# The products of the recurrence that read q ahead of those that read k, and one empty place in the queue of its steps

## The chip, the core and the metric

One core of a Trainium2 chip runs the whole program. The metric is the device time of one execution in microseconds (us), from the first to the last instruction with the little that stands around them; lower is better. The engines work side by side and wait for each other through semaphores: PE is TensorE (matmuls; PEld are its weight loads), DVE is VectorE, ACT is ScalarE, POOL is GpSimd, and SP issues most of the DMAs.

## The reference: what is computed

One layer of a decoder trunk runs for a prompt (256 rows) and for 8 samples of 8 rows (64 rows); they share all weights. The layer projects the normalized input to q, k, v, gates and a pooling branch, runs gated linear attention with 4 heads, merges both branches, projects back, and ends with a SwiGLU feed-forward part. What the change touches is the gated linear attention:

```
b = jnp.cumsum(loga, axis=3)
b_last = b[:, :, :, -1:, :]
qe = q * jnp.exp(b)
ke = k * jnp.exp(-b)
kd = k * jnp.exp(b_last - b)
decay = jnp.exp(b_last[:, :, :, 0, :])
...
att = jnp.where(mask, jnp.einsum('nbhcd,nbhsd->nbhcs', qe, ke), 0.0)
o_intra = jnp.einsum('nbhcs,nbhse->nbhce', att, v)
...
s = dec_n[..., None] * s + jnp.einsum('bhcd,bhce->bhde', kd_n, v_n)
```

## The kernel before

All 320 rows (256 of the prompt, 64 of the samples) stand in the free dimension. Each weight chunk of 128x512 numbers is loaded by SP (`raw`), split into a high part by ACT (`whi`, L159) and a low part by DVE (`wlo`, L160), and each weight tile then takes three matmuls of 320 columns (`mm3`, L198 to L200). `whi` and `wlo` have five buffers each. A projection (`proj`) covers 256 output columns: 96 such matmuls into one PSUM tile of the pool `pmain`, which has two buffers (`ps`, and `psy` for the pooling branch). A PSUM tile comes free when `evac` has copied it into SBUF or added it to what is there (DVE L383 for group 0's gates `mg`). Four more PSUM tiles (`pmisc`, `pm`) serve everything else.

The four heads are done as groups h = 0 to 3. While the projections of group h+1 run on PE, the recurrence of group h is slipped in between them: its steps are functions in a list, and `pump(10)` calls the next ten of them after each projection unit. For group 0 the list is: the gates (`sig0`), four steps of the pooling branch, the first 12 steps of `gla_steps`, the pooling product `s_y`, and the rest. `PSY` is the number of steps ahead of `s_y`. The order of the calls is not the last word: a scheduler then moves instructions on each engine by its own estimates, except where code pins them.

The steps that matter here: `s_gk` makes the log of the gate (ACT L774 to L782, DVE L780 and L783); `s_exp(d)`, d = 0 and 1 for the two halves of a head, sums it over time with six matmuls (L795 and L796, into `pa` and `pb`) and takes nine exponentials on ACT (L800 to L805); `s_prod` multiplies them with q and k on DVE (L811 to L833) and lets POOL copy part of the k products (L816). `s_vstack` stacks v (ACT L841, DVE L843), `s_nat2`, `s_nat3` and `s_kp` transpose on PE (L132, L136). `s_y` multiplies the pooled rows by their weights into two `psy` tiles, which DVE adds at L1090.

q and k of all groups live in one buffer each. So the copy of the next group's q out of PSUM (`evac`, ACT L385) has to wait until DVE has done the last product that reads the old q, and until it is done its PSUM tile is not free. In between, `ada_step` multiplies modulation weights (`w_ada`) in sets of 32 or 48 small matmuls (L250).

Of the kernel before, what the change touches and what calls it, by code (L numbers as in the profile page):

```python
# [15 lines left out]
ALU = mybir.AluOpType  # L16
# [4 lines left out]
P = 128  # L21
TP, NB, LS = 256, 8, 8
TS = NB * LS
T = TP + TS
# [8 lines left out]
OQ, OK_, OV, OOG, OU, OGA, OGB, OAL = 0, 1024, 2048, 4096, 6144, 7168, 9216, 11264  # L33
UEP = PB + TP
UEW = UEP + NB * (PB + LS)
PSY = 12
WB = 5
AB = 3
SLICES = ((0, 2), (2, 4), (4, 8), (8, 12), (12, 16))
# [42 lines left out]
def body(tc, A):  # L82
# [22 lines left out]
    V, S, G, PE = nc.vector, nc.scalar, nc.gpsimd, nc.tensor  # L105
# [222 lines left out]
    def s3(ap):  # L328
        return ap.rearrange("p (b t) -> p b t", t=LS)
# [414 lines left out]
    def w4(shape, dt=F32):  # L744
        return lp.tile(shape, dt, tag="w4", bufs=4, name=nm("w4"))

    def gla_steps(g):
        h = g.h
        st = []
# [39 lines left out]
        def s_exp(d):  # L789
            def f():  # L790
                pa, pb = misc(), misc()
                ds = slice(d * P, (d + 1) * P)
                for ps, rows, s, rhs, a, b in ((pa, P, 0, M0, 0, NM0), (pa, TS, 2, MS, NM0, NM0 + NMS),
                                               (pb, P, 1, M1, 0, NM1)):
                    PE.matmul(ps[:, a:b], lhsT=E["lgh"][:rows, s, ds], rhs=rhs, start=True, stop=False)  # L795
                    PE.matmul(ps[:, a:b], lhsT=E["lgl"][:rows, s, ds], rhs=rhs, start=False, stop=True)  # L796
                EQ, EK, EX = E["EQ"][:, d], E["EK"][:, d], E["EX"][:, d]
                i16 = 1.0 / 16.0
                for dst, sc in ((EQ, i16), (EK, -i16)):
                    S.activation(dst[:, 0:P], pa[:, 0:P], AF.Exp, scale=sc)  # L800
                    S.activation(dst[:, P:2 * P], pb[:, 0:P], AF.Exp, scale=sc)
                    S.activation(dst[:, TP:T], pa[:, NM0:NM0 + TS], AF.Exp, scale=sc)
                S.activation(EX[:, 0:144], pa[:, P:NM0], AF.Exp, scale=i16)
                S.activation(EX[:, 144:416], pb[:, P:NM1], AF.Exp, scale=i16)
                S.activation(EX[:, 416:480], pa[:, NM0 + TS:NM0 + 2 * TS], AF.Exp, scale=i16)  # L805
            return f

        def s_prod():
            EQ, EK, EX, q, k = E["EQ"], E["EK"], E["EX"], g.q, g.k
            for d in range(2):  # L810
                V.tensor_tensor(qeP[:, d, :, 0:LS], s3(EQ[:, d, TP:T]), s3(q[:, d, TP:T]), op=ALU.mult)  # L811
                kk = s3(k[:, d, TP:T])
                V.tensor_tensor(keP[:, d, :, 0:LS], s3(EK[:, d, TP:T]), kk, op=ALU.mult)
                V.tensor_copy(E["dec"][:, d], s3(EQ[:, d, TP:T])[:, :, LS - 1])
            for d in range(2):
                G.tensor_copy(keP[:, d].rearrange("p b (c t) -> p b c t", t=LS)[:, :, 1:4, :],  # L816
                              keP[:, d, :, 0:LS].unsqueeze(2).broadcast_to([P, NB, 3, LS]))
            V.tensor_tensor(EX[:, :, 416:480], EX[:, :, 416:480], k[:, :, TP:T], op=ALU.mult)
            kdP = E["kdP"] = w4([P, 2, NB, 32], F32R)
            for d in range(2):  # L820
                kd4 = kdP[:, d].rearrange("p b (c t) -> p b c t", t=LS)
                kd = s3(EX[:, d, 416:480]).unsqueeze(2).broadcast_to([P, NB, 2, LS])
                V.tensor_copy(kd4[:, :, 0:2, :], kd)
                V.tensor_tensor(kd4[:, :, 2:4, :], kd, kd4[:, :, 0:2, :].bitcast(F32), op=ALU.subtract)
            V.tensor_tensor(EQ[:, :, 0:TP], EQ[:, :, 0:TP], q[:, :, 0:TP], op=ALU.mult)
            V.tensor_tensor(EK[:, :, 0:TP], EK[:, :, 0:TP], k[:, :, 0:TP], op=ALU.mult)
            kq = w4([P, 2, 2, P])
            E["kdA"], E["q2"] = kq[:, 0], kq[:, 1]
            V.tensor_tensor(EX[:, :, 0:P], EX[:, :, 0:P], k[:, :, 0:P], op=ALU.mult)
            V.tensor_tensor(EX[:, :, 144:272], EX[:, :, 144:272], k[:, :, P:TP], op=ALU.mult)  # L830
            V.tensor_tensor(E["q2"], EX[:, :, 272:400], q[:, :, P:TP], op=ALU.mult)
            for d in range(2):
                V.tensor_scalar(E["kdA"][:, d], EX[:, d, 0:P], EX[:, d, 399:400], None, op0=ALU.mult)  # L833

# [113 lines left out]
        def s_load(gg, d):  # L948
            def f():
                t = lp.tile([P, 4, DV], F32, tag="S0", bufs=2, name=nm("S0"))  # L950
                nc.gpsimd.dma_start(t, A["state_gla"][0, 4 * gg:4 * gg + 4, h, d * P:(d + 1) * P, :]
                                    .rearrange("b p e -> p b e"))
                E["S0", gg, d] = t
            return f
# [36 lines left out]
        def s_norm():  # L991
# [11 lines left out]
            V.reciprocal(rs, rs)  # L1003
            for e in range(4):
                V.scalar_tensor_tensor(o[:, e], o[:, e], GNG[:, e:e + 1], rs, op0=ALU.mult, op1=ALU.mult)
        st += [s_load(0, 0), s_load(0, 1), s_wa2, s_gk, s_exp(0), s_exp(1), s_prod, s_vstack, s_nat2, s_nat3, s_kp(0), s_attP,
               s_inter(0), s_oback(0)]
        for d in range(2):
            st += [s_state(0, d, 0), s_state(0, d, 2), s_load(1, d)]
# [90 lines left out]
        return f  # L1100

    queue = []

    def pump(n):
        for _ in range(min(n, len(queue))):
# [278 lines left out]
```

## Time and profile before

| | |
|---|---|
| median of 3 runs | 1969.22 us (1968.83 to 1969.24) |
| the profiled execution | 1966.94 us, of which the span of instructions is 1965.2 us |
| PE busy | 1938.0 us, 99% of the span |
| DVE, ACT, POOL busy | 1020.0, 826.4, 137.4 us |
| mean granted clock of PE | 0.996 of full speed |

PE is the engine to look at: what the others do matters only where PE stands still for it, or runs at the lower clock. A busy PE is counted by modelled ends of its matmuls, so the spacing of starts says more than a busy share. The profiled execution is 2.3 us shorter than the median of the runs.

### The profile page before, as it was taken

How to read it: one execution, taken by the hardware profiler on the slowest of the kernel's cores; microseconds unless marked ns; L12 is line 12 of the kernel's file. 1: busy time of each engine (PE TensorE's matmuls, PEld its weight loads, DVE VectorE, ACT ScalarE, POOL GpSimd, SP SyncE). 2: the span in 40 equal slices, each digit the busy share in tenths (PEclk: the TensorE clock that was granted, in tenths of full speed). 3: DMA queues.
4: the chain of work that ended last, by engine and by line, in shares of the span. 5: the costliest groups of instructions: out<-in, count | busy, mean ns of one | idle time of the engine just before them, and what ended most of it. 6: DMA issues, size and time to landing. Idle time of an engine off the chain costs nothing.

```text
span 1965.2 us, 37340 instructions
## 1 busy us (share of the span) xinstructions
PE 1938.0 (99%) x15068; PEld 1850.7 (94%) x15068; DVE 1020.0 (52%) x1912; ACT 826.4 (42%) x1493; POOL 137.4 (7%) x257
## 2 busy tenths in 40 slices
PE   9999999999999999999999999999999999999997
PEld 6899998898999999889999999999999999999997
DVE  3666575565556544774574444444444444444554
ACT  4333374463345433643353333333333434344443
POOL 1012220111011101010030000000000000000000
PEclk9999999999999999999999999999999999999998
DMA  9988645765976786679656765444444444444443
GB/s 320 398 274 267 193 143 181 260 229 201 324 240 207 277 267 217 207 253 329 205 186 195 224 195 187 148 152 143 154 151 150 150 150 151 150 150 144 148 140 94
DMA packets 324607, 400.84 MB, mean 204 GB/s; under 512 B 13545, under 2 KB 264681, under 8 KB 324097
## 3 DMA queue, kind: packets, MB, share of 16 engines
q1 hardware_dynamic: 312002, 357.68, 56.4%
q0 software_dynamic: 12432, 40.78, 5.7%
q8 instruction: 118, 1.93, 0.4%
q14 instruction: 55, 0.45, 0.1%
HBM read 373.96 MB, written 24.67 MB: 203 GB/s over the span
## 4 chain that ended last, share of the span: by engine, by line
PE 92%; ACT 1%; DMA 1%; DVE 1%; issue 0%; POOL 0%; POOLq 0%; DVEq 0%; ACTq 0%
PE ps L198 27%; PE ps L199 27%; PE ps L200 27%; PE pm L250 4%; PE pm L132 1%; PE pm L963 1%; PE pm L984 1%; DMA raw<-w_ada 1%; PE pm L928 1%; PE pm L917 0%; PE pm L795 0%; PE pm L136 0%; PE pm L796 0%; PE pm L863 0%; PE psy L198 0%
## 5 line engine op out<-in xcount | busy, mean ns | idle before, releaser
L160 DVE TENSOR_TENSOR wlo<-raw,whi 128x512 fp32r<-128x512 f32 x948 | 653.9, 694 | 770.2 <-ACT whi L159 766.8
L159 ACT CAST whi<-raw 128x512 fp32r<-128x512 f32 x948 | 584.7, 621 | 972.1 <-PE ps L199 869.2
L198 PE MATMUL ps<-hh,whi 128*128 128x320 f32 x1408 | 440.8, 314 | 3.2 <-ACT hh L572 1.0
L200 PE MATMUL ps<-hh,wlo 128*128 128x320 f32 x1408 | 438.5, 312 | 0.1
L199 PE MATMUL ps<-hl,whi 128*128 128x320 f32 x1408 | 437.4, 311 | 0.7 <-DVE hl L588 0.7
L198 PE MATMUL ps<-h2h,whi 128*128 128x320 f32 x1408 | 435.8, 310 | 0.0
L199 PE MATMUL ps<-h2l,whi 128*128 128x320 f32 x1408 | 434.9, 309 | 0.8 <-DVE h2l L1254 0.8
L200 PE MATMUL ps<-h2h,wlo 128*128 128x320 f32 x1408 | 434.8, 309 | 0.0
L198 PEld LDWEIGHTS ps<-hh,whi 128*128 128x128 f32 x1408 | 264.3, 188 | 19.5 <-issue 11.9
L199 PEld LDWEIGHTS ps<-hl,whi 128*128 128x128 f32 x1408 | 264.4, 188 | 7.1 <-issue 4.6
L200 PEld LDWEIGHTS ps<-hh,wlo 128*128 128x128 f32 x1408 | 264.4, 188 | 6.2 <-issue 4.9
L198 PEld LDWEIGHTS ps<-h2h,whi 128*128 128x128 f32 x1408 | 264.1, 188 | 2.4 <-issue 2.2
L199 PEld LDWEIGHTS ps<-h2l,whi 128*128 128x128 f32 x1408 | 264.3, 188 | 1.1 <-DVE h2l L1254 1.1
L200 PEld LDWEIGHTS ps<-h2h,wlo 128*128 128x128 f32 x1408 | 264.3, 188 | 0.0
L198 PE MATMUL ps<-ah,whi 128*128 128x320 f32 x704 | 218.5, 310 | 0.0
L200 PE MATMUL ps<-ah,wlo 128*128 128x320 f32 x704 | 217.7, 309 | 0.0
L199 PE MATMUL ps<-al,whi 128*128 128x320 f32 x704 | 217.6, 309 | 0.0
L199 PEld LDWEIGHTS ps<-al,whi 128*128 128x128 f32 x704 | 132.2, 188 | 0.0
L198 PEld LDWEIGHTS ps<-ah,whi 128*128 128x128 f32 x704 | 132.2, 188 | 0.0
L200 PEld LDWEIGHTS ps<-ah,wlo 128*128 128x128 f32 x704 | 132.2, 188 | 0.0
L250 PE MATMUL pm<-raw,scT 128*32 128x128 f32 (+1 forms) x2688 | 99.5, 290 | 0.3 <-DMA raw<-w_ada 0.3
L250 PEld LDWEIGHTS pm<-raw,scT 128*32 128x32 f32 x2688 | 71.0, 109 | 21.1 <-issue 13.6
(321 smaller groups left out, 1581.4 us busy)
## 6 DMA issues: line engine op xcount, KB each, us to landing
raw<-w_ada SPq DMA_DIRECT2D x192, 512.0 KB, 6.4
raw<-w_gu SPq DMA_DIRECT2D x176, 512.0 KB, 3.5
raw<-w_in SPq DMA_DIRECT2D x173, 512.0 KB, 4.1
raw<-w_down SPq DMA_DIRECT2D x79, 512.0 KB, 3.3
S<-state_gla POOLq DMA_DIRECT2D x16, 1024.0 KB, 8.9
o_gs<-S POOLq DMA_DIRECT2D x16, 1024.0 KB, 5.9
raw<-w_o SPq DMA_DIRECT2D x32, 512.0 KB, 5.3
raw<-w_down SPq DMA_DIRECT2D x15, 256.0 KB, 2.6
```

The source lines that it names most:

```text
L132: PE.transpose(out, in_, ident[:k, :k])
L159: S.copy(hi, raw)
L160: V.tensor_sub(lo, raw, hi.bitcast(F32))
L198: PE.matmul(ps, lhsT=whi, rhs=xhi, start=start, stop=False)
L199: PE.matmul(ps, lhsT=whi, rhs=xlo, start=False, stop=False)
L200: PE.matmul(ps, lhsT=wlo, rhs=xhi, start=False, stop=stop)
L250: ins = PE.matmul(ps[32 * j:32 * j + 32, 0:w], lhsT=scT[:, k, :], rhs=raws[j], start=k == 0 if start is None else start, stop=k == KT - 1 ...
L928: PE.matmul(pt, lhsT=E["kdn"][:, s, d * P:(d + 1) * P], rhs=E["vn"][:, s], start=s == 0, stop=s == 1)
L963: PE.matmul(pt[32 * j:32 * j + 32, :], lhsT=qeP[:, d, 4 * gg + j, :], rhs=E["S0", gg, d][:, j], start=False, stop=d == 1, tile_position=(0 ...
L984: PE.matmul(pt, lhsT=kpz[:, j, d * P:(d + 1) * P], rhs=E["vp"][:, gg], start=True, stop=True)
```

## The change

In `s_prod` the copy of the decays (`dec`) and the four products with q are called first, then those with k. The list of steps of every group gets an empty step (`pause`) behind `s_gk`, and `PSY` goes from 12 to 13, so that `s_y` of group 0 keeps its place among the steps. Since the tenth step of group 0's list was `s_exp(0)`, this step, and one at each later border of ten, is now called one projection later. For the groups 1 to 3 the whole list is called between two projections, so there the empty step moves nothing by itself.

```diff
@@ -33,7 +33,7 @@
 OQ, OK_, OV, OOG, OU, OGA, OGB, OAL = 0, 1024, 2048, 4096, 6144, 7168, 9216, 11264
 UEP = PB + TP
 UEW = UEP + NB * (PB + LS)
-PSY = 12
+PSY = 13
 WB = 5
 AB = 3
 SLICES = ((0, 2), (2, 4), (4, 8), (8, 12), (12, 16))
@@ -807,11 +807,16 @@
 
         def s_prod():
             EQ, EK, EX, q, k = E["EQ"], E["EK"], E["EX"], g.q, g.k
+            kq = w4([P, 2, 2, P])
+            E["kdA"], E["q2"] = kq[:, 0], kq[:, 1]
             for d in range(2):
+                V.tensor_copy(E["dec"][:, d], s3(EQ[:, d, TP:T])[:, :, LS - 1])
                 V.tensor_tensor(qeP[:, d, :, 0:LS], s3(EQ[:, d, TP:T]), s3(q[:, d, TP:T]), op=ALU.mult)
+            V.tensor_tensor(EQ[:, :, 0:TP], EQ[:, :, 0:TP], q[:, :, 0:TP], op=ALU.mult)
+            V.tensor_tensor(E["q2"], EX[:, :, 272:400], q[:, :, P:TP], op=ALU.mult)
+            for d in range(2):
                 kk = s3(k[:, d, TP:T])
                 V.tensor_tensor(keP[:, d, :, 0:LS], s3(EK[:, d, TP:T]), kk, op=ALU.mult)
-                V.tensor_copy(E["dec"][:, d], s3(EQ[:, d, TP:T])[:, :, LS - 1])
             for d in range(2):
                 G.tensor_copy(keP[:, d].rearrange("p b (c t) -> p b c t", t=LS)[:, :, 1:4, :],
                               keP[:, d, :, 0:LS].unsqueeze(2).broadcast_to([P, NB, 3, LS]))
@@ -822,13 +827,9 @@
                 kd = s3(EX[:, d, 416:480]).unsqueeze(2).broadcast_to([P, NB, 2, LS])
                 V.tensor_copy(kd4[:, :, 0:2, :], kd)
                 V.tensor_tensor(kd4[:, :, 2:4, :], kd, kd4[:, :, 0:2, :].bitcast(F32), op=ALU.subtract)
-            V.tensor_tensor(EQ[:, :, 0:TP], EQ[:, :, 0:TP], q[:, :, 0:TP], op=ALU.mult)
             V.tensor_tensor(EK[:, :, 0:TP], EK[:, :, 0:TP], k[:, :, 0:TP], op=ALU.mult)
-            kq = w4([P, 2, 2, P])
-            E["kdA"], E["q2"] = kq[:, 0], kq[:, 1]
             V.tensor_tensor(EX[:, :, 0:P], EX[:, :, 0:P], k[:, :, 0:P], op=ALU.mult)
             V.tensor_tensor(EX[:, :, 144:272], EX[:, :, 144:272], k[:, :, P:TP], op=ALU.mult)
-            V.tensor_tensor(E["q2"], EX[:, :, 272:400], q[:, :, P:TP], op=ALU.mult)
             for d in range(2):
                 V.tensor_scalar(E["kdA"][:, d], EX[:, d, 0:P], EX[:, d, 399:400], None, op0=ALU.mult)
 
@@ -1003,7 +1004,7 @@
             V.reciprocal(rs, rs)
             for e in range(4):
                 V.scalar_tensor_tensor(o[:, e], o[:, e], GNG[:, e:e + 1], rs, op0=ALU.mult, op1=ALU.mult)
-        st += [s_load(0, 0), s_load(0, 1), s_wa2, s_gk, s_exp(0), s_exp(1), s_prod, s_vstack, s_nat2, s_nat3, s_kp(0), s_attP,
+        st += [s_load(0, 0), s_load(0, 1), s_wa2, s_gk, pause, s_exp(0), s_exp(1), s_prod, s_vstack, s_nat2, s_nat3, s_kp(0), s_attP,
                s_inter(0), s_oback(0)]
         for d in range(2):
             st += [s_state(0, d, 0), s_state(0, d, 2), s_load(1, d)]
@@ -1100,6 +1101,9 @@
         return f
 
     queue = []
+
+    def pause():
+        pass
 
     def pump(n):
         for _ in range(min(n, len(queue))):
```

How the scheduler places it is seen at two places of group 0's recurrence. The first is on PE, after the gate projection `ps_3000`: the names are PSUM tiles and what is multiplied into them, `cumr` the matrix of the sums and `w` the log of the gate.

```order
 L199 MATMUL ps_3000<-hl_2626,whi_3019 128x320
 L200 MATMUL ps_3000<-hh_106,wlo_3020 128x320
-L795 MATMUL pm_3326<-cumr,w_490_3309 128x272
-L796 MATMUL pm_3326<-cumr,w_491_3310 128x272
-L795 MATMUL pm_3326<-cumr,w_490_3309 128x128
-L795 MATMUL pm_3327<-cumr,w_490_3309 128x400
-L796 MATMUL pm_3327<-cumr,w_491_3310 128x400
 L198 MATMUL ps_3036<-hh_103,whi_3039 128x320
 L199 MATMUL ps_3036<-hl_2524,whi_3039 128x320
```

The five sums of `s_exp(0)` that stood between the projections `ps_3000` and `ps_3036` are gone; a sixth, 48 matmuls on, is gone too. All twelve sums of both halves now stand at the second place, ahead of and between the pooling products. There PE had, before the change (in brackets the engines whose semaphores a row waits for):

```order
L198 MATMUL psy_3621<-dh_3289,whi_3641 128x320
L199 MATMUL psy_3621<-dl_3290,whi_3641 128x320
L200 MATMUL psy_3621<-dh_3289,wlo_3642 128x320
L198 MATMUL psy_3622<-dh_3289,whi_3625 128x320 [waits PE_49,Activation_49]
L199 MATMUL psy_3622<-dl_3290,whi_3625 128x320
L200 MATMUL psy_3622<-dh_3289,wlo_3626 128x320
```

and has now (`pm_3523` is `pb` of the second half):

```order
L198 MATMUL psy_3621<-dh_3289,whi_3641 128x320
L199 MATMUL psy_3621<-dl_3290,whi_3641 128x320
L200 MATMUL psy_3621<-dh_3289,wlo_3642 128x320
L795 MATMUL pm_3523<-cumr,w_490_3309 128x400 [waits PE_49,Activation_49]
L796 MATMUL pm_3523<-cumr,w_491_3310 128x400
L198 MATMUL psy_3622<-dh_3289,whi_3625 128x320 [waits DVE_49]
L199 MATMUL psy_3622<-dl_3290,whi_3625 128x320
L200 MATMUL psy_3622<-dh_3289,wlo_3626 128x320
```

The last two sums stand between the two pooling tiles, and the second tile `psy_3622` no longer waits for ACT but for DVE, so it takes the buffer that `psy_3621` leaves. DVE had at this place, in the second half of the products:

```order
L811 TENSOR_TENSOR qeP<-EQK_3323,q_248 128x8x8 [waits Activation_49]
L814 COPY dec_3324<-EQK_3323 128x8
L813 TENSOR_TENSOR keP<-EQK_3323,k_249 128x8x8 [waits Activation_49]
L829 TENSOR_TENSOR EX_3325<-EX_3325,k_249 128x2x128 [waits Activation_49]
L818 TENSOR_TENSOR EX_3325<-EX_3325,k_249 128x2x64 [waits Activation_49]
L825 TENSOR_TENSOR EQK_3323<-EQK_3323,q_248 128x2x256 [waits Activation_49]
L826 TENSOR_TENSOR EQK_3323<-EQK_3323,k_249 128x2x256 [waits Activation_49]
L830 TENSOR_TENSOR EX_3325<-EX_3325,k_249 128x2x128 [waits Activation_49]
L823 CAST w_531_3548<-EX_3325 128x8x16 [waits DVE_49]
L823 CAST w_531_3548<-EX_3325 128x8x16
L831 TENSOR_TENSOR w_532_3555<-EX_3325,q_248 128x256
L833 TENSOR_SCALAR w_532_3555<-EX_3325 128x128 x2
```

and has now:

```order
L813 COPY dec_3324<-EQK_3323 128x8 [waits Activation_49]
L814 TENSOR_TENSOR qeP<-EQK_3323,q_248 128x8x8
L819 TENSOR_TENSOR keP<-EQK_3323,k_249 128x8x8 [waits Activation_49]
L831 TENSOR_TENSOR EX_3325<-EX_3325,k_249 128x2x128 [waits Activation_49]
L823 TENSOR_TENSOR EX_3325<-EX_3325,k_249 128x2x64 [waits Activation_49]
L1091 SCALAR_TENSOR_TENSOR mg_111<-psy_3621,vec,mg_111 128x320 [waits PE_49]
L1091 SCALAR_TENSOR_TENSOR mg_111<-psy_3621,vec,mg_111 128x320
L834 TENSOR_SCALAR w_531_3539<-EX_3325 128x128 [waits DVE_49]
L815 TENSOR_TENSOR EQK_3323<-EQK_3323,q_248 128x2x256 [waits Activation_49]
L830 TENSOR_TENSOR EQK_3323<-EQK_3323,k_249 128x2x256 [waits Activation_49]
L816 TENSOR_TENSOR w_531_3539<-EX_3325,q_248 128x256 [waits Activation_49]
L828 CAST w_532_3551<-EX_3325 128x8x16 [waits DVE_49]
```

The two instructions that empty `psy_3621` (L1091, L1090 before) now stand ahead of the large products with q, and the last product that reads q (L816, L831 before) stands ahead of the casts (L828, L823 before) and of one product with k, behind which it stood. ACT had, in the same stretch,

```order
L801 ACTIVATE EQK_3323<-pm_3523 128x128 [waits PE_49]
L801 ACTIVATE EQK_3323<-pm_3523 128x128
L804 ACTIVATE EX_3325<-pm_3523 128x272
L841 CAST w_533_3561<-v_250 128x8x8 x8
L385 ACTIVATE q_3343<-ps_3347 128x640 [waits DVE_49]
L159 CAST whi_3735<-raw_3717 128x512 [waits PE_49,Activation_49]
```

and has now

```order
L801 ACTIVATE EQK_3323<-pm_3523 128x128 [waits PE_49]
L801 ACTIVATE EQK_3323<-pm_3523 128x128
L804 ACTIVATE EX_3325<-pm_3523 128x272
L842 CAST w_533_3561<-v_250 128x8x8 x8
L159 CAST whi_3724<-raw_3706 128x512 [waits DVE_49,PE_49]
L385 ACTIVATE q_3326<-ps_3330 128x640 [waits DVE_49]
```

The copy of q out of PSUM (L385) stands behind one more split of weights (L159), whose buffer is the one that `psy_3622` reads.

## Rows read from the trace of the kernel before

**Rows 1.** The page: engine totals, and two groups by line (busy us, mean ns).

```profile
PE 1938.0 (99%) x15068; PEld 1850.7 (94%) x15068; DVE 1020.0 (52%) x1912; ACT 826.4 (42%) x1493; POOL 137.4 (7%) x257
L160 DVE TENSOR_TENSOR wlo<-raw,whi 128x512 fp32r<-128x512 f32 x948 | 653.9, 694 | 770.2 <-ACT whi L159 766.8
L159 ACT CAST whi<-raw 128x512 fp32r<-128x512 f32 x948 | 584.7, 621 | 972.1 <-PE ps L199 869.2
```

**Rows 2.** PE's waits in the whole span: us in total, times, longest.

```profile
PE psy L198 <- ACT q L385: 2.3, 1, 2.3
PE pm L796 <- DVE w L783: 1.4, 1, 1.4
PE pm L795 <- ACT w L782: 0.8, 1, 0.8
```

**Rows 3.** Timeline of PE, 268 to 280 us (start, us, instruction).

```profile
268.57 0.31 PE L200 MATMUL ps<-hh,wlo 128*128 128x320 f32 x1
271.69 0.31 PE L198 MATMUL ps<-hh,whi 128*128 128x320 f32 x1
278.58 0.31 PE L200 MATMUL ps<-hh,wlo 128*128 128x320 f32 x1
279.07 0.41 PE L198 MATMUL ps<-hh,whi 128*128 128x320 f32 x1
```

**Rows 4.** Timeline of POOL and DVE, 267 to 272 us.

```profile
267.89 1.55 POOL L401 TENSOR_TENSOR og<-og,sg 128x640 f32<-128x640 f32 x1 [4.16 <-ACT sg L397]
268.35 1.64 DVE L160 TENSOR_TENSOR wlo<-raw,whi 128x512 fp32r<-128x512 f32 x1 [1.86 <-ACT whi L159]
270.51 0.81 DVE L383 SCALAR_TENSOR_TENSOR mg<-ps,mg 128x640 f32<-128x640 f32 x1
```

**Rows 5.** Windows (length, busy by engine, PEclk, DMA share, GB/s).

```profile
272.00:276.00 4.00, 4.00 (x29) 4.00 (x29) 2.22 (x5) 3.96 (x8) 0.50 (x1) 1.00 0.72 223
311.00:314.00 3.00, 3.00 (x14) 3.00 (x14) 2.54 (x13) 0.86 (x2) 0.00 (x0) 0.59 0.12 44
314.00:316.00 2.00, 2.00 (x14) 2.00 (x14) 2.00 (x4) 0.39 (x1) 0.00 (x0) 0.76 0.59 158
```

**Rows 6.** Timeline of PE, 305 to 315 us.

```profile
305.36 0.39 PE L795 MATMUL pm<-cumr,w 128*128 128x272 f32 x1
306.64 0.31 PE L198 MATMUL psy<-dh,whi 128*128 128x320 f32 x1
308.26 0.30 PE L200 MATMUL psy<-dh,wlo 128*128 128x320 f32 x1
310.89 0.42 PE L198 MATMUL psy<-dh,whi 128*128 128x320 f32 x1 [2.33 <-ACT q L385]
314.80 0.46 PE L198 MATMUL ps<-hh,whi 128*128 128x320 f32 x1
```

**Rows 7.** Timeline of ACT and DVE, 305 to 315 us.

```profile
306.28 0.28 ACT L800 ACTIVATE EQK<-pm 128x128 f32<-128x128 f32 x1 [0.49 <-PE pm L796]
307.09 0.51 ACT L801 ACTIVATE EQK<-pm 128x128 f32<-128x128 f32 x2
307.68 1.33 ACT L841 CAST w<-v 128x64 fp32r<-128x64 f32 x8
307.88 0.68 DVE L825 TENSOR_TENSOR EQK<-EQK,q 128x512 f32<-128x512 f32 x1
309.69 0.41 DVE L831 TENSOR_TENSOR w<-EX,q 128x256 f32<-128x256 f32 x1
310.13 0.70 ACT L385 ACTIVATE q<-ps 128x640 f32<-128x640 f32 x1 [1.12 <-DVE w L831]
313.99 1.01 DVE L1090 SCALAR_TENSOR_TENSOR mg<-psy,vec,mg 128x320 f32<-128x320 f32 x2 [0.46 <-PE psy L200]
```

**Rows 8.** Waits of the SP queue in the whole span.

```profile
SPq L149 <- PE pm L250: 61.1, 71, 3.2
```

**Rows 9.** DMA issues of the page: count, KB, median us to landing.

```profile
raw<-w_in SPq DMA_DIRECT2D x173, 512.0 KB, 4.1
```

## The prediction

> **What bounds the kernel.** I read the page first: PE is busy for 1938.0 us, 99% of the span, and no other engine for more than 52% [rows 1]. So only two things can move the time: moments in which PE stands still, and moments in which it runs at its lower clock. The list of PE's waits has three entries in the stretch that the change touches: 2.3 us before the second pooling tile, 1.4 us before a sum of the decays, 0.8 us before the same sums of group 1 [rows 2]. Then the timelines around the two places of group 0, and windows over them for the clock.
>
> At the second place the last matmul of the first pooling tile starts at 308.26 and the first of the second at 310.89 [rows 6]. Twelve matmuls from 306.64 to 308.26 are eleven spacings: 0.147 us each at full clock. So 2.63 - 0.15 = 2.48 us are lost. The chain behind it: PE's sums, ACT's exponentials from 306.28, the DVE products until 310.10 (309.69 + 0.41), the copy of q until 310.83, PE at 310.89 [rows 6, 7]. [...] At the first place PE stood for 1.4 us, and the clock in 272 to 276 stayed at 1.00 [rows 2, 5].
>
> **First place: the sums that leave.** Before, the last matmul of one gate projection starts at 268.57 and the next projection at 271.69, with five sums and the wait of 1.4 us in between [rows 2, 3]. After, nothing stands in between; but the next projection needs the PSUM buffer that DVE empties at L383, and that ends at 270.51 + 0.81 = 271.32 [rows 4]. What comes ahead of it on DVE, ACT and POOL is not changed by the edit. So PE starts at about 271.36 and wins 0.33 us, not 1.4: the wait is renamed, and PE now stands from 268.72 to 271.36, 2.64 us, with no sums to fill it. The lone sixth sum goes too: 279.07 - 278.58 = 0.49 us, against a spacing of 0.15, wins 0.34 [rows 3]. Together 0.67. The supply of weight tiles behind it does not get worse: by the order on ACT, two loads of activation tables between the splits are gone.
>
> **Second place: the sums that arrive.** Count from the first of the twelve sums. Six took 306.64 - 305.36 = 1.28 us [rows 6], so twelve and the first pooling tile (12 x 0.147 = 1.76) keep PE until 4.32. The last two sums stand behind the tile, which therefore ends near 4.0 (an estimate: a third of 1.28 earlier, and the drain).
>
> ACT starts 0.92 after the first sum (306.28 - 305.36) and needs 307.68 - 306.28 = 1.40 for nine exponentials; the second half starts at 2.32. DVE's large products began 1.60 after ACT's start (307.88 - 306.28) [rows 7], so here DVE is through its small ones at 3.92. It then empties the first pooling tile, two instructions of 1.01 us together [rows 7], until 5.05, and the second tile starts: PE waits 5.05 - 4.32 = 0.73, and is done at 6.81.
>
> The copy of q comes later. ACT's last three exponentials need the last sums (4.32, with drain 4.5) and take 307.68 - 307.09 = 0.59; the eight casts of v take 1.33, the split of weights that now stands ahead 0.62, the copy itself 0.70 [rows 1, 7]: 4.5 + 0.59 + 1.33 + 0.62 + 0.70 = 7.74. The q products don't decide: from the first large product to the end of the last one with q were 2.22 us (307.88 to 310.10, [rows 7]), less some 0.4 for what now stands behind, so 5.05 + 1.8 = 6.9, ahead of the copy at 7.04. **The order of q and k, which the change is named after, is worth nothing here**, since ACT is later than DVE. The next projection starts at 7.75 and waits 0.94.
>
> In the same count the kernel before took 314.80 - 305.36 = 9.44 us [rows 6], with six of the sums and with six transposes that now come later. Those ran mostly at the lower clock, 1.05 us from the end of the pooling tile; at full clock at least half of that, I take 0.6. So 7.75 + 0.6 = 8.35, and the place wins 1.09, the fall of the clock that goes with the gap included. Bounds of the waits: 0 if DVE and ACT are faster than counted; the old 2.48 if they are as late as before.
>
> **Group 1.** Ahead of its sums stand 39 projection matmuls where 31 stood. Eight times 0.147 is 1.2 us more cover for a wait of 0.8 [rows 2]. ACT has one more sigmoid in front of the gate, hidden in part. Between 0 and 0.8 I take 0.75. The groups 2 and 3 have no PE wait that the new order could take away; there nothing is counted, since the q copy is a whole group away.
>
> **The clock at the first place.** This is the disputed cost: 0 or 1.71. Idle for 2.3 us was followed by a fall, 1.4 us was not [rows 2, 5]. A standstill of 2.64 between starts is nearest to the one of 2.48, so I take the fall: it moves from the second place, where the two waits are short and have work between them, to the first.
>
> [...] The subtraction at 268.35 took 1.64 us, against 694 ns on average, while POOL multiplied from 267.89 for 1.55 us [rows 1, 4]. POOL's two copies of the k products now follow each other closer to the critical chain; I count nothing for it, since the chain of [rows 7] already had one beside it; if a product is stretched as this one was, that is 1.64 - 0.69 = 0.95 us more (a rival below). [...]
>
> **The sum.** 0.67 + 1.09 + 0.75 - 1.71 = 0.8 us faster, against 1966.94 us of the profiled execution: 1966.1. That execution is 2.3 us under the median of the runs, 1969.22, so on the scale of the runs 1968.4. A measurement of this kernel can tell about 0.2%, 3.9 us, from no change; this is inside.
>
> **The rivals.**
> - No fall at either place: gain 2.5, 1966.7 us. For it: 1.4 us did not bring one. Against: the standstill is the longest in the stretch.
> - Falls at both places: 0.9 slower, 1970.1. For it: 0.73 + 0.94 us of waiting lie close together. Against: each alone is shorter than 1.4.
> - Slower by more than can be missed: the sets of modulation matmuls move by up to 36 projection matmuls in group 1 (5.3 us later), and SP, which issues in order, holds the weight loads queued behind theirs. It waited 71 times for such a set, 3.2 us at the longest [rows 8]. A load lands in 4.1 us [rows 9]; 5.3 + 4.1 = 9.4 against a cover of two other buffers, 2 x 24 x 0.147 = 7.1: 2.3 us short for one set. Eight sets move later; two of them decide (4.7 us, 1973.1). Against it: the order of SP's loads moves along with the sets.
> - Faster by more than can be missed: no fall, and ACT and DVE early enough that both waits at the second place are gone: 2.5 + 1.67 = 4.2, 1965.0. Against it: the copy of q stands behind a split that itself waits for the second pooling tile.
> - POOL in the way: one product on the chain is stretched by 0.95 us [rows 1, 4], the time 1969.4. Against it: one such copy ran beside the old chain, and its times are those used here.
> - The change does not do what it says: that is in the sum already; the gain comes from the place in the queue alone.
>
> **Numbers.** My forecast 0.45, no fall 0.23, falls at both 0.13, slow loads 0.08, all waits gone 0.07, POOL in the way 0.04. The first three lie from 1966.7 to 1970.1; with half of either tail and 1 us for how an execution stands to the runs: 1965.4 to 1971.0. Faster by over 0.2%: 0.1 (all waits gone, and a part of no fall); slower by over 0.2%: 0.09; within: 0.81.
>
> **What the profile after would show.** Right: a PE wait for DVE's L383 near 268.7 to 271.4 with the clock low just behind it; waits of under 1 us each before the second pooling tile (for DVE L1091) and before the next projection (for ACT L385), with the clock at 1.00; none before group 1's L795. Wrong: a wait on L385 as long as the old one; a projection that waits for a load; a clock of 1.00 throughout.

## The result, and the profile after

| | before | after |
|---|---|---|
| median of 15 runs | 1968.1 us (1966.47 to 1971.07) | 1972.95 us (1969.83 to 1976.71) |
| ratio, 95% interval | | 1.0023 (1.0016 to 1.003) |
| the profiled execution | 1966.94 us, span 1965.2 | 1973.64 us, span 1971.9 |

The changed kernel is slower by a little more than the 0.2% that a measurement of this kernel can tell, and 1972.95 lies outside the range that was given, 1965.4 to 1971.0. PE is still the whole of it: 1940.3 us busy, where it was 1938.0 [rows 1]. Its waits in the changed kernel (us in total, times, longest), of those that answer to [rows 2] and one that had hardly been there:

```profile
PE pm L250 <- DMA raw<-w_ada: 5.5, 3, 3.8
PE ps L198 <- DVE mg L383: 2.6, 1, 2.6
PE psy L198 <- DVE mg L1091: 0.7, 1, 0.7
PE pm L795 <- ACT w L782: 0.7, 1, 0.7
PE ps L198 <- ACT q L385: 0.4, 1, 0.4
```

Three of these lines the prediction named as they came; that for L795 was to be gone. The first it did not see: a set of modulation matmuls (L250) waits for a load of its weights, 3.8 us at the longest; before, such waits came to 0.3 us. The timeline of PE in the changed kernel (start, us, instruction, in brackets the idle time ahead of it):

```profile
271.09 0.39 PE L198 MATMUL ps<-hh,whi 128*128 128x320 f32 x1 [2.58 <-DVE mg L383]
...
305.91 0.39 PE L795 MATMUL pm<-cumr,w 128*128 128x272 f32 x1
...
311.03 0.42 PE L198 MATMUL psy<-dh,whi 128*128 128x320 f32 x1 [0.74 <-DVE mg L1091]
...
313.50 0.42 PE L198 MATMUL ps<-hh,whi 128*128 128x320 f32 x1 [0.45 <-ACT q L385]
...
400.69 2.79 PE L250 MATMUL pm<-raw,scT 128*32 128x128 f32 x48 [3.80 <-DMA raw<-w_ada]
403.41 0.64 PE L199 MATMUL ps<-hl,whi 128*128 128x320 f32 x1
```

and windows over it (length; busy us of PE, PEld, DVE, ACT and POOL, each with its instructions; PEclk, DMA share, GB/s):

```profile
268.00:272.00 4.00, 1.42 (x10) 1.18 (x9) 4.00 (x6) 2.31 (x5) 1.05 (x1) 1.00 0.29 72
272.00:276.00 4.00, 4.00 (x19) 4.00 (x18) 2.50 (x4) 1.89 (x3) 0.79 (x1) 0.58 0.62 194
300.00:311.00 11.00, 10.29 (x103) 9.13 (x102) 5.33 (x15) 6.30 (x23) 0.87 (x2) 1.00 0.68 214
311.00:320.00 9.00, 8.52 (x59) 8.26 (x60) 8.68 (x27) 5.22 (x16) 0.00 (x0) 1.00 0.39 117
396.00:399.00 3.00, 0.90 (x7) 0.64 (x5) 0.00 (x0) 0.00 (x0) 1.83 (x4) 0.98 1.03 404
399.00:401.00 2.00, 0.30 (x8) 0.29 (x12) 0.62 (x2) 1.27 (x3) 0.00 (x0) 0.50 1.08 385
403.00:406.00 3.00, 3.00 (x22) 2.61 (x15) 2.97 (x4) 0.32 (x1) 0.00 (x0) 0.54 0.84 214
```

At the places of group 0 the kernel does what was forecast: the long standstill and the low clock are at the first place, 272 to 276, where [rows 5] had 1.00; at the second place, 300 to 320, the clock is at 1.00 and two short waits are left. New is the standstill at 397 to 401, with the DMA engines fully taken (1.03 to 1.08, where the kernel before has 1.04 to 1.06) and the granted clock at 0.50 from 399 to 401 and at 0.54 from 403 to 406. The kernel before had, in the same windows and for the same set:

```profile
396.00:399.00 3.00, 3.00 (x23) 2.99 (x22) 2.36 (x6) 0.59 (x1) 1.89 (x5) 1.00 1.04 407
399.00:401.00 2.00, 2.00 (x15) 1.89 (x13) 1.93 (x5) 0.00 (x0) 1.31 (x2) 1.00 1.06 380
```

```profile
401.09 1.52 PE L250 MATMUL pm<-raw,scT 128*32 128x128 f32 x48
```

The standstill costs 3.8 us, then 2.79 us for a set of 48 matmuls that takes 1.52 at full clock (so it did in the kernel before), then some 2.6 us at 0.54: 3.8 + 1.27 + 1.2 = 6.3.

To see which stretch the time went to, one can follow the splits of weights (DVE L160), which come in one order in both kernels. From the 105th of the 948 (start 262.83 before, 262.45 after) to the 149th (369.77, 369.32) lie the two places of group 0: 106.9 us in either kernel. From the 149th to the 233rd (563.91, 568.67) lies the new wait: 194.1 us before, 199.4 after. So these 84 splits cost 5.2 us of the 6.7 by which the span grew (1971.9 - 1965.2), 1.1 less than the 6.3 summed up above. On PE itself, the 60 projection matmuls (L198 to L200) on either side of the set's new place take 19.82 us before and 26.06 after, 6.2 more, with the same other matmuls among them; in the 992 behind these, with the same other work again, 1.0 us is won back, 0.3 of it in waits. Where the rest of it comes from isn't traced. Behind that another 1.8 us are lost (233rd to 601st split: 763.8 us before, 765.6 after); the run that has only the new order of the products and every set at its old place (below) takes 766.0 there, so that isn't the moved set. Most of it is one more wait for w_ada, 1.16 us at 903.05, which the trace of the kernel before doesn't have and that run's has (1.66 us at 899.88).

Why does the set wait? By the order on PE it now stands 26 projection matmuls earlier (26 x 0.147 = 3.8 us). Its loads on SP's queue, which go off as the set ahead of it (383.14) gives back the three buffers ([rows 8] are SP's waits of this kind), in the changed kernel:

```profile
378.67 0.37 SPq L149 DMA_DIRECT2D raw<-w_in  x1
383.84 0.88 SPq L149 DMA_DIRECT2D raw<-w_ada  x2
384.82 2.41 SPq L149 DMA_DIRECT2D raw<-w_in  x1
387.28 1.24 SPq L149 DMA_DIRECT2D raw<-w_ada  x1
```

A set multiplies its three chunks in the reverse order of their loads, so it waits first for the last one, sent off at 387.28 and landed at 400.69, 13.4 us later. In the kernel before the three loads went off together, between 385.27 and 388.87, and the set at 401.09 did not wait:

```profile
385.27 3.60 SPq L149 DMA_DIRECT2D raw<-w_ada  x3
```

Now the set is due 3.8 us earlier, its last load goes off at about the same time (387.28, where it was 387.43), and the wait is 3.8 us: the kernel before had next to nothing to spare there. This is worked out, since the landing of its third load is not in the trace: 13.4 us behind 387.43 would be 400.8 (an estimate), and the set started at 401.09.

### The profile page after: what moved, and what is told of

Same layout as the page of the kernel before. It is cut to its first block, busy times and chain, and to the rows that moved or that the text cites. A ratio compares the mean times of both kernels' runs of the same rounds, so it can differ in the third digit from the quotient of the medians.

```text
span 1971.9 us, 37338 instructions
## 1 busy us (share of the span) xinstructions
PE 1940.3 (98%) x15068; PEld 1853.4 (94%) x15068; DVE 1016.8 (52%) x1912; ACT 821.6 (42%) x1489; POOL 137.9 (7%) x257
## 4 chain that ended last, share of the span: by engine, by line
PE 91%; DMA 2%; ACT 1%; DVE 1%; issue 0%; POOL 0%; POOLq 0%; SPq 0%; ACTq 0%; DVEq 0%
PE ps L198 27%; PE ps L199 27%; PE ps L200 27%; PE pm L250 4%; DMA raw<-w_ada 1%; PE pm L132 1%; PE pm L964 1%; PE pm L985 1%; PE pm L929 1%; DMA raw<-w_o 0%; PE pm L918 0%; PE pm L136 0%; PE pm L795 0%; PE pm L864 0%; PE pm L796 0%
## 5 line engine op out<-in xcount | busy, mean ns | idle before, releaser
L160 DVE TENSOR_TENSOR wlo<-raw,whi 128x512 fp32r<-128x512 f32 x948 | 653.1, 693 | 772.7 <-ACT whi L159 754.2
L159 ACT CAST whi<-raw 128x512 fp32r<-128x512 f32 x948 | 584.8, 620 | 978.1 <-PE ps L199 866.2
L198 PE MATMUL ps<-hh,whi 128*128 128x320 f32 x1408 | 442.7, 315 | 4.8 <-DVE mg L383 2.6
L200 PE MATMUL ps<-hh,wlo 128*128 128x320 f32 x1408 | 440.4, 313 | 0.1
L198 PE MATMUL ps<-h2h,whi 128*128 128x320 f32 x1408 | 435.8, 310 | 0.0
L200 PE MATMUL ps<-h2h,wlo 128*128 128x320 f32 x1408 | 434.9, 309 | 0.0
L198 PEld LDWEIGHTS ps<-hh,whi 128*128 128x128 f32 x1408 | 265.8, 189 | 21.8 <-issue 13.2
L200 PEld LDWEIGHTS ps<-hh,wlo 128*128 128x128 f32 x1408 | 266.1, 189 | 7.3 <-issue 5.9
L198 PEld LDWEIGHTS ps<-h2h,whi 128*128 128x128 f32 x1408 | 264.1, 188 | 2.4 <-issue 2.2
L200 PEld LDWEIGHTS ps<-h2h,wlo 128*128 128x128 f32 x1408 | 264.3, 188 | 0.0
L198 PE MATMUL ps<-ah,whi 128*128 128x320 f32 x704 | 218.5, 310 | 0.0
L200 PE MATMUL ps<-ah,wlo 128*128 128x320 f32 x704 | 217.7, 309 | 0.0
L198 PEld LDWEIGHTS ps<-ah,whi 128*128 128x128 f32 x704 | 132.2, 188 | 0.0
L200 PEld LDWEIGHTS ps<-ah,wlo 128*128 128x128 f32 x704 | 132.2, 188 | 0.0
L250 PE MATMUL pm<-raw,scT 128*32 128x128 f32 (+1 forms) x2688 | 101.0, 293 | 5.5 <-DMA raw<-w_ada 5.5
L250 PEld LDWEIGHTS pm<-raw,scT 128*32 128x32 f32 x2688 | 72.0, 110 | 27.0 <-issue 12.9
```

What stands on the lines that cost most here:

```text
L159: S.copy(hi, raw)
L160: V.tensor_sub(lo, raw, hi.bitcast(F32))
L198: PE.matmul(ps, lhsT=whi, rhs=xhi, start=start, stop=False)
L200: PE.matmul(ps, lhsT=wlo, rhs=xhi, start=False, stop=stop)
L250: ins = PE.matmul(ps[32 * j:32 * j + 32, 0:w], lhsT=scT[:, k, :], rhs=raws[j], start=k == 0 if start is None else start, stop=k == KT - 1 ...
```

## Experiments

**Theory A**: the set that comes earlier waits for a load that has no slack, and the clock falls behind that wait. **Theory B**: the new order of the products on DVE. **Theory C**: the first and the second place of group 0, as the change rearranged them.

### Each half of the change alone

```diff
-PSY = 12
+PSY = 13
...
-        st += [s_load(0, 0), s_load(0, 1), s_wa2, s_gk, s_exp(0), s_exp(1), s_prod, s_vstack, s_nat2, s_nat3, s_kp(0), s_attP,
+        st += [s_load(0, 0), s_load(0, 1), s_wa2, s_gk, pause, s_exp(0), s_exp(1), s_prod, s_vstack, s_nat2, s_nat3, s_kp(0), s_attP,
```

> The kernel before with the empty step and PSY = 13 alone; the products of s_prod stand in their old order. Theory A (the sets of modulation matmuls: the empty step makes the scheduler put one set 26 projection matmuls earlier, it waits 3.8 us for its last load, and the clock falls behind it): as the changed kernel, 1.0023 of the kernel before, with a PE wait of 3 to 4 us for w_ada near 397 to 401 us and a granted clock near 0.7 in 400 to 410. Theory B (the new order of the products on DVE holds something up): 1.000, and no such wait. Theory C (the rearranged first and second places of group 0, with the 2.6 us wait and the fall behind it): 1.002 too, but with a wait for w_ada below 1 us.

Measured: 1.0015 (1.0007 to 1.0024). PE's timeline shows the same wait, and the same low clock (48 matmuls in 2.79 us):

```profile
400.52 2.79 PE L250 MATMUL pm<-raw,scT 128*32 128x128 f32 x48 [3.46 <-DMA raw<-w_ada]
```

The other half is the order of `s_prod` alone, on the kernel before (the first lines of it):

```diff
             for d in range(2):
+                V.tensor_copy(E["dec"][:, d], s3(EQ[:, d, TP:T])[:, :, LS - 1])
                 V.tensor_tensor(qeP[:, d, :, 0:LS], s3(EQ[:, d, TP:T]), s3(q[:, d, TP:T]), op=ALU.mult)
+            V.tensor_tensor(EQ[:, :, 0:TP], EQ[:, :, 0:TP], q[:, :, 0:TP], op=ALU.mult)
+            V.tensor_tensor(E["q2"], EX[:, :, 272:400], q[:, :, P:TP], op=ALU.mult)
...
```

> The kernel before with the new order of the products in s_prod alone; no empty step, PSY = 12. Theory A (the sets): the sets stand where they stood before, so 1.000 (0.999 to 1.001), waits for w_ada near 0.3 us in all, and the PE wait for ACT L385 before the second pooling tile stays near 2.3 us. Theory B (the order of the products costs the time): 1.002. Theory C (the places of group 0): 1.000, as for A.

Measured: 0.9996 (0.9987 to 1.0005). Its waits on PE:

```profile
PE pm L250 <- DMA raw<-w_ada: 2.5, 3, 1.7
...
PE psy L198 <- ACT q L385: 1.9, 1, 1.9
```

The empty step alone makes the kernel slower, the order of the products doesn't: B falls. The wait for the copy of q shrinks by 0.4 us, from 2.3 to 1.9; that is all that the order brings where the old queue is kept. The 2.5 us of waits for w_ada (0.3 was expected) do not lie at 400, where the window 396 to 400 has PE busy for 4.00 of 4.00; they are 0.48 us at 521.76, 0.32 at 679.40 and 1.66 at 899.88.

### The set back at its place, and an extra buffer

The changed kernel, with one line of `ada_pump`:

```diff
-        if ada_acc[0] >= 1.0 and len(ada_done) < ada_acc[2]:
+        if ada_acc[0] >= 1.0 + (0.25 if len(ada_done) == 3 else 0.0) and len(ada_done) < ada_acc[2]:
```

> The changed kernel, in which one set of modulation matmuls (the fourth of its stretch) is asked for one chunk of a projection later, 24 matmuls; the order on PE then has this set, all later ones and group 1's sums where the kernel before has them, and the first and second places of group 0 as the change made them. Theory A (the sets): the wait of 3.8 us and the low clock behind it are gone, about 7 us of the profile after; 0.9995 of the kernel before (0.999 to 1.0003), with the waits for L383 (2.6), L1091 (0.7) and L385 (0.4) still there. Theory C (the places of group 0 cost the time): 1.002, as the changed kernel.

Measured: 0.9995 (0.9987 to 1.0004). SP sends the three loads off together again, and the set starts with no wait:

```profile
386.91 3.12 SPq L149 DMA_DIRECT2D raw<-w_ada  x3
```

```profile
402.72 1.52 PE L250 MATMUL pm<-raw,scT 128*32 128x128 f32 x48
```

The waits for L383, L1091 and L385 are there with 2.6, 0.7 and 0.4 us, as in the changed kernel, and the time is that of the kernel before. C falls: the loss is not at the places of group 0.

The changed kernel with a fourth buffer:

```diff
-AB = 3
+AB = 4
```

> The changed kernel with four buffers for the modulation weights in place of three (AB = 4). The set stands at the same place (30 projection matmuls earlier than in the kernel before), but the load for which it waited can be sent off one buffer sooner. Theory A1 (it waits because its last load is sent off too late, when the third buffer comes free): the wait of 3.8 us goes below 1 us and the time is 1.000 of the kernel before (0.999 to 1.001). Theory A2 (the transfers are too crowded around 384 to 400 us, whatever buffer is free): a wait of 2 us or more stays and the time is near 1.002. Theory C (the places of group 0): 1.002 without that wait.

Measured: 1.0027 (1.0016 to 1.0038). The set does not wait any more (it starts at 401.43, its splits 149 to 233 take 194.5 us), as A1 has it; but the time is not that of A1, since 5 us are lost earlier. With the fourth buffer SP sends off four loads of w_ada in a row near 230 us, not three; behind that (the link between the two isn't shown) PE waits 1.23 us at 250 and 0.87 at 268, and at the first place 3.93 us, with the clock low for longer:

```profile
275.54 0.60 PE L198 MATMUL ps<-hh,whi 128*128 128x320 f32 x1 [3.93 <-DVE mg L383]
```

```profile
272.00:276.00 4.00, 0.46 (x2) 0.49 (x3) 2.44 (x5) 3.97 (x7) 0.00 (x0) 0.78 0.37 115
276.00:280.00 4.00, 4.00 (x17) 4.00 (x17) 2.76 (x5) 3.31 (x5) 0.00 (x0) 0.50 0.52 152
```

### An early set in the kernel before, and other mends

The kernel before, with the third set asked for later:

```diff
-        if ada_acc[0] >= 1.0 and len(ada_done) < ada_acc[2]:
+        if ada_acc[0] >= 1.0 + (0.25 if len(ada_done) == 2 else 0.0) and len(ada_done) < ada_acc[2]:
```

> The kernel before, recurrence untouched, with one edit to the modulation sets: the third set of the stretch is asked for one chunk of a projection later. By the order on PE the next two then stand 12 and 30 projection matmuls earlier than in the kernel before, with 82 matmuls between them (100 in the kernel before, 77 in the changed kernel), and all later ones and group 1's sums about where the changed kernel has them. Theory A (the sets alone cost the time): 1.002 of the kernel before (1.001 to 1.003), with a PE wait of 2 to 4 us for w_ada near 396 to 401 us and a low clock behind it, while the old wait of 2.3 us for ACT L385 at the second place stays. Theory C (the rearranged recurrence costs it): 1.000 and no such wait.

Measured: 1.0006 (0.9997 to 1.0014); the wait is 0.91 us, at 397.37, and no low clock follows. A is not confirmed as it was put: the set is 30 matmuls early and costs hardly anything. On SP its three loads go off between 383.22 and 385.58, with nothing in between; the last of them some 2 us earlier than in the changed kernel. So it is not the place of the set alone, but the time between the last load and the set.

The changed kernel with the chunks of a set in forward order:

```diff
-        todo = [(c, j) for c in reversed(range(c0, c1)) for j in range(2)]
+        todo = [(c, j) for c in range(c0, c1) for j in range(2)]
```

> The changed kernel, in which a modulation set multiplies its chunks in the order in which they are loaded, not in the reverse of it. The early set stands at the same place to 4 matmuls (30 earlier than in the kernel before); later sets are cut into smaller pieces. Theory A with the reason that the set waits first for the chunk that was sent off last: two thirds of the set (2 x 0.93 us) run before that chunk is needed, so the 3.8 us wait falls by 1.9 or more and the time is 1.001 of the kernel before (1.000 to 1.002). If all three chunks land late together, the wait stays at 3 us or more and the time is 1.002.

Measured: 1.0057 (1.0045 to 1.0069), a miss. Two thirds of the set do run first, at 396.08, but the last third waits just as long, for the same load:

```profile
400.80 0.65 PE L250 MATMUL pm<-raw,scT 128*32 128x128 f32 x16 [3.64 <-DMA raw<-w_ada]
```

and the later sets, cut into pieces, add 4 us of their own (splits 149 to 233 take 203.2 us). The load lands at 400.80 here and at 400.69 in the changed kernel, with the two orders of use.

The changed kernel without two stores of states:

```diff
-                if j0 == 2:
+                if j0 == 2 and not (h == 0 and gg == 0):
```

> The changed kernel without the two stores of the new states of the first four samples of group 0 (1 MB each, issued at 378 and 383 us); that part of o_gs isn't written. The order on PE keeps every set where the changed kernel has it. Theory A2 (the load of the early set lands some 12 us after its issue because the stores and loads of the states take the DMA engines in 378 to 400): the load lands several us sooner, the 3.8 us wait falls below 1 us, the clock stays up in 400 to 410, and the time is 0.999 of the kernel before (0.998 to 1.000). Theory A1 (it is sent off too late, whatever else is under way): the wait stays above 2.5 us and the time at 1.0015 to 1.0025.

Measured: 1.0008 (0.9999 to 1.0017), with a wait of 3.30 us. This run does not test what it was meant to: the stores that it leaves out are those that the changed kernel issues at 340 and 347 us; its trace shows the two others still, at 376.90 and 381.87. The third load goes off at 385.35 and the set starts at 398.36, 13.0 us later. Its interval takes in 1, although wait and low clock are there and its splits 149 to 233 take 198.1 us; with the first two stores gone and no low clock at the first place (table below), its whole time says little on the wait. The right pair was left out in the last run, below.

The changed kernel with the fourth set asked for two chunks later:

```diff
-        if ada_acc[0] >= 1.0 and len(ada_done) < ada_acc[2]:
+        if ada_acc[0] >= 1.0 + (0.5 if len(ada_done) == 3 else 0.0) and len(ada_done) < ada_acc[2]:
```

> The changed kernel, in which the fourth set is asked for two chunks of a projection later, not one. By the order on PE the two sets then stand 22 and 11 projection matmuls later than in the kernel before, all later ones as there. As a version that may beat both: the waits for w_ada near 400 us go from 1.2 to nearly 0, the second place of group 0 keeps its gain; 0.999 of the kernel before (0.998 to 1.000). If the sets that come later now wait in their turn, it is 1.000.

Measured: 1.0004 (0.9996 to 1.0013). The set at 404.68 still waits 1.12 us, since its loads go off later too (390.23 to 392.30). No version that beats both.

### The two sides of the slack, one at a time

The changed kernel, in which only the waiting set is asked for one chunk later:

```diff
-        if ada_acc[0] >= 1.0 and len(ada_done) < ada_acc[2]:
+        if ada_acc[0] >= 1.0 + (0.25 if len(ada_done) == 4 else 0.0) and len(ada_done) < ada_acc[2]:
```

> The changed kernel, in which only the set that waits (the fifth of its stretch) is asked for one chunk of a projection later. By the order on PE it then stands 20 projection matmuls later than in the changed kernel, 6 earlier than in the kernel before; on SP a load of projection weights still stands between the second and the third of its three loads, as in the changed kernel. If the moment at which the set needs its load decides: 20 x 0.147 = 2.9 us of the 3.8 us wait go, 0.9 is left, no low clock behind it, and the time is 1.000 of the kernel before (0.999 to 1.001). If the load is simply stuck behind the one in between, the wait stays above 2.5 us and the time at 1.002.

Measured: 0.9996 (0.9987 to 1.0005). SP's queue is as in the changed kernel, the load between included; the load goes off at 387.38 and lands at 401.02; the set, 20 matmuls later, waits only for the rest:

```profile
384.91 2.41 SPq L149 DMA_DIRECT2D raw<-w_in  x1
387.38 1.19 SPq L149 DMA_DIRECT2D raw<-w_ada  x1
```

```profile
401.02 1.51 PE L250 MATMUL pm<-raw,scT 128*32 128x128 f32 x46 [1.09 <-DMA raw<-w_ada]
```

The other side: the loads go off earlier and the set stays early, by the same edit of the changed kernel that the kernel before was given above (`0.25 if len(ada_done) == 2`):

```diff
-        if ada_acc[0] >= 1.0 and len(ada_done) < ada_acc[2]:
+        if ada_acc[0] >= 1.0 + (0.25 if len(ada_done) == 2 else 0.0) and len(ada_done) < ada_acc[2]:
```

> The changed kernel, in which the third set of the stretch is asked for one chunk later. By the order on PE the fourth set then stands 20 projection matmuls earlier than in the changed kernel and the fifth, the one that waits, 4 earlier, so still 30 before its place in the kernel before; on SP its three loads now follow each other with nothing in between. If the moment of the issue decides (the third load is sent off 20 x 0.147 = 2.9 us earlier, and about 2.5 us earlier again for the load that no longer stands in between): the wait of 3.8 us falls below 1 us although the set is as early as in the changed kernel, and the time is 1.000 of the kernel before (0.999 to 1.001). If the place of the set decides by itself, the wait stays above 2.5 us and the time at 1.002.

Measured: 0.9997 (0.9986 to 1.0008).

```profile
379.04 3.43 SPq L149 DMA_DIRECT2D raw<-w_ada  x3
```

```profile
395.09 1.52 PE L250 MATMUL pm<-raw,scT 128*32 128x128 f32 x48 [0.86 <-DMA raw<-w_ada]
```

Moving either end by some 3 us takes the loss away, and in both the clock stays at 1.00 from 396 to 410. Then the waiting set two chunks later in place of one:

```diff
-        if ada_acc[0] >= 1.0 and len(ada_done) < ada_acc[2]:
+        if ada_acc[0] >= 1.0 + (0.5 if len(ada_done) == 4 else 0.0) and len(ada_done) < ada_acc[2]:
```

> The changed kernel, in which only the set that waits is asked for two chunks of a projection later: 44 projection matmuls behind its place in the changed kernel, 18 behind that in the kernel before; group 1's sums come at about the place of the kernel before. As a version that may beat both: its wait is 0 (44 x 0.147 = 6.5 us against 3.8), nothing behind it is late, and the gain at the places of group 0 stays; 0.999 of the kernel before (0.998 to 1.000).

Measured: 0.9997 (0.9989 to 1.0005). The set at 404.90 doesn't wait at all. It is the clean mend of the changed kernel, and no faster than the kernel before: what the change wins is below what a measurement can tell.

At last the stores that lie beside the load:

```diff
-                if j0 == 2:
+                if j0 == 2 and not (h == 0 and gg == 1):
```

> The changed kernel without the two stores of group 0's new states that its trace shows at 378 and 383 us (the last four samples; that part of o_gs isn't written). The run without the first four samples' stores had left out those at 340 and 347 us instead, and still showed the two at 377 and 382 us. On PE the waiting set, and on SP its three loads with one load in between, stand as in the changed kernel; two MB of the four that POOL's queue moves between 378 and 396 us are gone. If that traffic is why the third load needs 13 us: it lands at least 3 us sooner, the 3.8 us wait falls below 1 us, no low clock behind it, and the time is 0.9995 of the kernel before (0.998 to 1.000). If it isn't: the wait stays above 2.5 us and the time at 1.0015 to 1.0025.

Measured: 0.999 (0.9981 to 1.0). The set starts at 397.37 without a wait, though its third load went off at 386.68 with the other load ahead of it, so it landed within 10.7 us:

```profile
397.37 1.52 PE L250 MATMUL pm<-raw,scT 128*32 128x128 f32 x48
```

The edit also moves what is left: the next two loads of states go off at 378.87 and 383.85, some 7 us earlier than in the changed kernel (385.54 and 390.78). The DMA queues from 384 to 401 us (packets, MB, share of the 16 engines; q0 is POOL's, q1 SP's), in the changed kernel and in this run:

```profile
q0 software_dynamic: 892, 3.29, 55.0%
q1 hardware_dynamic: 2191, 2.94, 46.8%
```

```profile
q1 hardware_dynamic: 3191, 4.05, 70.0%
q0 software_dynamic: 381, 1.30, 20.8%
```

With 2 MB less on POOL's queue in these 17 us (1.30 in place of 3.29) SP's loads take 70.0% of the engines, where they took 46.8%, and move 4.05 MB in place of 2.94. How the engines choose between the two queues is not shown. This run writes less than the reference does, so it is no version to use.

### All runs in one table

The waiting set and its cost, and the places of group 0. The stretches are those of the 105th, 149th and 233rd split, worked out from their starts as above. The ratio is that of all executions, the other columns are those of the one that was traced for each kernel.

| run | ratio | wait of the set, us | splits 105 to 149, us | clock at the first place | splits 149 to 233, us |
|---|---|---|---|---|---|
| before | 1 | 0 | 106.9 | 1.00 (fall at the second) | 194.1 |
| after | 1.0023 | 3.80 | 106.9 | falls | 199.4 |
| empty step alone | 1.0015 | 3.46 | 107.2 | falls | 198.8 |
| new order alone | 0.9996 | 0 | 106.5 | 1.00 (fall at the second) | 194.9 |
| set back | 0.9995 | 0 | 105.3 | 1.00 | 195.5 |
| four buffers | 1.0027 | 0 | 108.4 | falls, twice as long | 194.5 |
| before, set early | 1.0006 | 0.91 | 107.2 | 1.00 (fall at the second) | 194.7 |
| chunks forward | 1.0057 | 3.64 | 106.9 | falls | 203.2 |
| stores at 340, 347 out | 1.0008 | 3.30 | 105.0 | 1.00 | 198.1 |
| both sets later | 1.0004 | 1.12 | 105.3 | 1.00 | 195.4 |
| set later, loads split | 0.9996 | 1.09 | 106.9 | falls | 196.2 |
| loads together | 0.9997 | 0.86 | 104.9 | 1.00 | 195.2 |
| set two later | 0.9997 | 0 | 106.6 | falls | 195.1 |
| stores at 378, 383 out | 0.999 | 0 | 106.0 | 1.00 | 193.9 |

Where the set waits 3.3 us or more the last stretch takes 198.1 us or more, in all other runs 193.9 to 196.2. The stretch from 105 to 149 holds the recurrence of group 0: there the prediction's own sum is tested.

## Why the prediction was wrong

**First place: right.** The wait was renamed, not removed: 2.58 us for L383, where 2.64 was counted (2.75 when it is counted from start to start, as the prediction did).

**Second place: right.** The second pooling tile waits 0.74 us for L1091 (0.73 counted), the next projection 0.45 us for L385 (0.94 counted). Both came with the clock at 1.00.

**The sum of both places: right, with the clock as an even chance.** Without a fall they were to win 0.67 + 1.09 = 1.76 us, with one next to nothing. In the table, among the runs with the changed queue and three buffers, those without a fall win 0.9 to 2.0 us against 106.9, those with a fall win or lose 0.4 at most. Starts on PE say it sharper, since splits can run ahead of it: from the last matmul in front of the first place to the 381st projection matmul behind it are 74.45 us before, 72.5 in each of the five without a fall, and 73.8 to 74.4 in the five with one. So the places win 1.9 us where 1.76 was counted, and, in the runs that have the new order of products, a fall costs 1.3 to 1.5. No run shows the 1.71 that the sum has for it: that is worked out from the clocks of [rows 5], 3 x 0.41 + 2 x 0.24, and the runs show these 1.3 to 1.5 in its place. The sum took the fall, by its nearest row, and gave it a chance of 0.45 against 0.23 for none; it came in five of ten.

**The order of q and k: nearly right.** Nothing was counted; over the same stretch of PE it is worth 0.4 us, with the old queue (74.45 to 74.03) as with the new one (74.40 to 74.05).

**POOL beside DVE: right to count nothing more.** The split beside POOL's L401 took 1.65 us again, at 267.96; the q products at the second place took 0.69 and 0.42 us, as in [rows 7].

**Group 1: wrong, and small.** The wait before its L795 is still 0.7 us; the 0.75 that eight more matmuls of cover were to bring did not come. That the wait moved along with ACT's chain, whatever stands in between, is likely and was not tested.

**The step that failed** is the third rival, "the sets of modulation matmuls move by up to 36 projection matmuls in group 1 (5.3 us later)", with a chance of 0.08; the sum gave nothing to the sets. It named the right resource and got three things wrong. It looked only at sets that move later, and asked whether SP is held up behind them; the set that mattered moves 26 matmuls earlier, at 397 us, and waits itself. It took a load as 4.1 us, the median of [rows 9]; in this stretch the DMA engines are taken to 1.03 and the load takes 13.4. And it set against itself that "the order of SP's loads moves along with the sets"; on SP a load of projection weights came to stand between the second and the third chunk (by itself that doesn't decide: it still stands there in the run with the set one chunk later, whose wait is 1.09 us). The trace of before holds what would have warned of it: the loads at 385.27 to 388.87, the set at 401.09, and a DMA share of 1.04 from 396 to 399. With next to no slack left, the move to an earlier place was paid in full, 3.8 us, and then once more by the clock, 1.27 + 1.2 us.

That the kernel's loss is this wait and the clock behind it is shown: it comes with the empty step alone, and goes when the set is later, when the load is earlier, or when half of the state traffic beside it is gone and the rest of it comes earlier. Why an empty step in group 0's list makes the scheduler put this set earlier was not followed up.

## What to carry to other kernels

When an edit makes a scheduler place its steps anew, look through the whole order for work that comes earlier and waits for a transfer, and compare for each the landing in the old trace with the new moment of need; what did not wait before may have had no slack. Take a transfer's time from the stretch where it runs, with the DMA share and the other queues beside it, not from the median over the program (13.4 us here, where the median of the loads of w_ada is 6.3). And a wait on the engine that bounds the kernel can cost more than its length: behind each of the five waits of 3.3 us or more in these traces the clock fell (0.50 to 0.83 in the windows of 2 to 10 us behind them).

## What was not expected of the hardware

The same standstill of PE, 2.6 us for L383 behind the same matmuls, was followed by the low clock in five traces (after, the empty step, the chunks forward, the set later, the set two later; 0.84 from 269 to 280 in each) and by none in five others (1.00). Nine of the ten programs have the same matmuls and the same instructions of DVE, ACT and POOL, in the same order, up to 305 us (in the tenth, the chunks forward, the sets use their chunks in another order). The windows of the run with the loads together, against the first two of the changed kernel above, differ in little but the clock, 1.00 in place of 0.58:

```profile
268.00:272.00 4.00, 1.41 (x10) 1.18 (x9) 4.00 (x6) 2.27 (x5) 1.02 (x1) 1.00 0.31 71
272.00:276.00 4.00, 4.00 (x30) 4.00 (x29) 3.29 (x6) 2.49 (x5) 0.83 (x1) 1.00 0.66 197
```

By the table the five with a fall take 106.9 us on average from the 105th to the 149th split, the five without 105.3: some 1.6 us. In the nine that are alike up to there, four with a fall and five without, no edit decides it, since each acts later. Each program was traced once, so how often one and the same program meets the fall is not shown. What decides it is not shown either. Waits of 2.3, 1.9 and 2.3 us at the old second place were followed by a fall in all three traces that have it (0.79 from 310 to 318 in each), and those of 3.3 us or more by one each time. The waits for w_ada of 0.86 to 1.16 us told here were followed by none (1.00 from 396 to 407, and in the changed kernel from 900 to 910), and the 1.4 us of the kernel before by none either (1.00 from 272 to 276). So the length of a wait does not decide by itself.
